# Attention output of a diffusion backbone: the two halves of a unit both copied by ScalarE and added on GpSimd

## Chip, core and metric

One core of one Trainium2 chip runs the whole program: TensorE (PE), VectorE (DVE), ScalarE (ACT), GpSimd (POOL), and SyncE (SP), which issues the DMAs. The metric is the device time of one execution in microseconds; three runs of the kernel before gave 2811.28 us as median (2810.51 to 2816.06).

## What is computed

Two layers over 512 latent tokens and 256 context tokens, 1024 wide. Each layer is a half-step SwiGLU, then three groups of heads side by side (GQA, a short gated convolution, MLA) between one input and one output projection, then another half-step SwiGLU; every sub-layer is modulated by a conditioning vector. The part that matters here is the attention, cut to its core:

```python
def one_block(qi):
    s = jnp.einsum('bhgqd,bhkd->bhgqk', qi, k).astype(jnp.float32) * scale
    p = jax.nn.softmax(s, axis=-1).astype(v.dtype)
    return jnp.einsum('bhgqk,bhkd->bhgqd', p, v)
```

There are 6 GQA heads and 6 MLA heads, each with values 64 wide. In layer 0 latent and context tokens are both queried, in layer 1 only the latent ones (`need_ctx`). All matrix products run in a split form: a float32 operand is held as a rounded high part and the remainder, and the products of the parts are summed.

## The kernel before

**Units.** The attention of a layer (`attend`, L1026) is a list of units: one head and two blocks of 128 queries. Layer 0 has three units a head (two of the latent tokens against all 768 keys, one of the context tokens against 256), so 36; layer 1 has two a head, so 24. A unit goes through these steps:

- `scores` (L945): queries times keys into a PSUM tile `ps`; `maxima` (L955): the row maximum, DVE, into a small tile `m`; `exps` (L960): ACT writes `t`, with the row sum.
- `transposes` (L967): PE turns the weights into PSUM tiles `po`; `high` (L985): ACT rounds them into `ph` or `s`; `low` (L998): DVE subtracts to get the remainder.
- `values` (L1007): PE multiplies by the values. The value operand holds a high and a low half side by side, so that the result `O`, a `po` tile of 128 partitions by 256, has the product with the high half in partitions 0 to 63 and that with the low half in 64 to 127.
- `out_copy` (L1014) and `out_add` (L1018) bring the two halves together: ACT copies partitions 64 to 127 of `O` into the tile `ot` of 64 by 256, and DVE adds it to partitions 0 to 63, read from PSUM, into the head's row `dest` of the mixed output (`mix`, an `s` tile).

Units overlap by three: in one turn of the loop the new unit's scores, the last one's transposes, the one before's `values` and the output of the one before that are issued. `jobs` hangs further work on given turns: `uq` and `ukv` (MLA's up projections, L1334 and L1362), `q_norm` and `k_norm` (L1408, L1427), `mla_part` (L1479), `mixnorm_a` and `mixnorm_b` (division by the row sums, L1457 and L1462) and `mix_split` (L1561).

**GpSimd's work in attention.** `q_norm` scales and rotates the MLA queries of all token tiles with seven GpSimd instructions for a latent tile and three for a context tile (L1417 to L1420, L1194, L1199, L1200), as soon as a chain of small DVE operations (`factors`, L1391) has made the scale `m`; `k_norm` does four more (L1432); `ukv` has short copies of the rotated key part `kr` (L1381); `mla_part` has the remainders `ql` and `s` (L1498), and `mix_split` those of the mixed rows (L1564).

**What sets the order.** In `attend` only TensorE is chained to program order (`chain("te")`, L1028). A scheduler places the instructions of ACT, DVE and POOL when the program is built, by its own estimate of when each may start; from then on every engine works through a fixed list in order. A tile with `bufs` buffers is written again when its last reader is done, and the writer waits for that by a semaphore. `ot` has two buffers (the tag is also used at the start by `wm0_copy`, L1639, for eight small copies), `po` has four, `ps` two.

**After the attention** come the output projection (`residual`, L373) and, beside it, the products for the modulation (`mod_steps`, L139; tiles `mr`, `mscr`) on DVE. Since helpers record most operations, their line is L65 in the profile.

Of the kernel before, what the change touches and what calls it, by code (L numbers as in the profile page):

```python
# [8 lines left out]
F32 = mybir.dt.float32  # L9
# [37 lines left out]
def tile_net(ctx: ExitStack, tc: tile.TileContext, a, out):  # L47
# [34 lines left out]
    te, ve, se, pe = Engine(nc.tensor, "te"), Engine(nc.vector, "ve"), Engine(nc.scalar, "se"), nc.gpsimd  # L82

    const = ctx.enter_context(tc.tile_pool(name="const", bufs=1))
    pool = ctx.enter_context(tc.tile_pool(name="pool", bufs=1))
# [4 lines left out]
    def nm(s):  # L90
        uid[0] += 1
        return f"{s}{uid[0]}"
# [4 lines left out]
    def temp(dt=F32, w=T):  # L97
        return pool.tile([P, w], dt, name=nm("t"), tag="t", bufs=NTMP)
# [838 lines left out]
    class Unit:  # L937
# [74 lines left out]
                te.matmul(out=self.O[:, :256], lhsT=self.V(kt), rhs=pl, start=False, stop=i == n - 1)  # L1012

        def out_copy(self):  # L1014
            self.tmp = pool.tile([64, 256], F32, name=nm("ot"), tag="ot", bufs=2)
            se.copy(self.tmp, self.O[64:128, :256])

        def out_add(self):  # L1018
            c = self.qbs[0] * P
            ve.tensor_add(self.dest[:, c:c + 256], self.O[0:64, :256], self.tmp)  # L1020

    class Nothing:
        def __getattr__(self, name):
# [576 lines left out]
    raws, parts, pms, sms = {}, {}, {}, {}  # L1600
# [36 lines left out]
                          start=kk == 0 and i == 0, stop=kk == KD - 1 and i == 1)  # L1637

    def wm0_copy(g):  # L1639
        sms[g] = pool.tile([64, 256], F32, name=nm("sm0"), tag="ot", bufs=2)  # L1640
        n = 2 if g in NATIVE else 4
        se.copy(sms[g][0:n, 0:256], pms[g][0:n, 0:256])

# [45 lines left out]
    Rs = pool.tile([P, D], F32, name="Rs", tag="mscr", bufs=1)  # L1689
    se.copy(Rs[:, LAT], Rl)  # L1690
    wm0_copy(0)
    wm0_high(1)
    for i in range(3):
        wm0_low(1, i)
    accs = []
    for g in range(KD):
        if g + 3 < KD:
            wm0_load(g + 3)
        if g:
            wm0_copy(g)  # L1700
        wm0_out(g)
        h.append((slot(F32R), slot(F32R)))
        cur = HMod(h[g], g, LAT, Rs, m01[1][:, g, 0:1], m01[0][:, g, 0:1], tv)
        cur.scaled()
        if g + 2 < KD:
            wm0_high(g + 2)
            cur.high()
            wm0_low(g + 2, 0)
            wm0_low(g + 2, 1)
            cur.low()  # L1710
            wm0_low(g + 2, 2)
        else:
            cur.high()
            cur.low()
        if g + 1 < KD:
            wm0_mm(g + 1)
        for j in PRE.get(g, ()):
            preload(j)
            accs.append(po())
        if g - 1 >= LAG:  # L1720
            for k in (range(g) if g - 1 == LAG else [g - 1]):
                for j in range(2):
                    lat_mm(accs[j], early[j], h, k, LAT, tv)
# [137 lines left out]
```

## Time and profile before

| | us |
|---|---|
| median of three runs | 2811.28 |
| the profiled execution | 2809.72 |
| its span | 2807.2 |
| first and last `ot` copy of layer 0 begin | 772.8, 953.3 |
| first and last `ot` copy of layer 1 begin | 2237.6, 2375.6 |
| POOL busy over the whole span | 189.6 |

The span is what the trace holds; 2.5 us lie around it. In a profile row stand the start and the length in us, the engine, the line, the operation, the tile written and the tiles read, and in square brackets how long the engine stood idle before it and who ended that. "Busy" counts the time in which an engine executes instructions. The chain of waits is followed back from the last instruction, at each step to what released it; its row by line gives the share of each kind of work on it.

### The profile page before, as it was taken

The page shows a single profiled execution, that of the slowest core. Times are in us where ns is not written, and L with a number is a line of the kernel's source. Part 1 is how long each engine was busy: PE and PEld are TensorE (multiplying, and loading weights), DVE is VectorE, ACT ScalarE, POOL GpSimd, SP SyncE. Part 2 cuts the span into 40 slices and gives each one's busy share as a digit, 9 for nine tenths or more (in the row PEclk, how much of TensorE's full clock was granted, in tenths as well). Part 3 has the DMA queues.
Part 4 walks back from the last instruction along what each step waited for, and adds up shares of the span by engine and source line. Part 5 has one row for each costly group of instructions (what it writes and reads, how often), then busy time and mean ns, then how long its engine had stood idle before and what let it go on. Part 6 is the DMA issues. An engine that isn't in the chain of part 4 may idle for free.

```text
span 2807.2 us, 38612 instructions
## 1 busy us (share of the span) xinstructions
PE 2691.4 (96%) x15188; PEld 2506.3 (89%) x15188; DVE 1983.7 (71%) x3391; ACT 1091.7 (39%) x1868; POOL 189.6 (7%) x225
## 2 busy tenths in 40 slices
PE   7999999989988999999999999999999899999999
PEld 4999999978878879999999899999988788888887
DVE  7657777787787887777777777776766888733333
ACT  5223333332477633333334333333333577422221
POOL 0000000011232210000000100000011233000000
PEclk9999999999999999999999999999999999999999
DMA  6423333224100331333333133333225101433232
GB/s 221 123 66 99 98 98 98 77 73 159 40 1 9 105 106 53 97 99 98 98 98 108 46 94 99 98 106 98 77 70 169 32 9 56 133 99 97 90 98 90
DMA packets 95461, 251.78 MB, mean 90 GB/s; under 512 B 11568, under 2 KB 41008, under 8 KB 95280
## 3 DMA queue, kind: packets, MB, share of 16 engines
q1 hardware_dynamic: 95280, 249.33, 28.6%
q8 instruction: 119, 1.95, 0.3%
q14 instruction: 62, 0.51, 0.1%
HBM read 247.19 MB, written 2.10 MB: 89 GB/s over the span
## 4 chain that ended last, share of the span: by engine, by line
PE 77%; DVE 12%; ACT 5%; DMA 3%; issue 2%; SPq 0%; POOL 0%; DVEq 0%; ACTq 0%
PE ps L65 45%; PE po L65 33%; DVE s L65 4%; DVE m L65 3%; ACT t L65 2%; ACT s L65 2%; DMA mr<-in_wm_dram 1%; DVE t L65 1%; DMA wr<-in_wiN_dram 1%; DVE wl L65 1%; DVE mr L65 1%; DVE mscr L65 1%; ACT ph L65 1%; DVE xT L65 0%; DMA s<-in_wm_dram 0%
## 5 line engine op out<-in xcount | busy, mean ns | idle before, releaser
L65 PE MATMUL ps<-s,wh 128*128 128x384 f32 (+2 forms) x4886 | 1185.5, 349 | 10.3 <-DVE xT L65 5.3
L65 PEld LDWEIGHTS ps<-s,wh 128*128 128x128 f32 x4886 | 868.8, 189 | 81.3 <-issue 5.7
L65 PE MATMUL ps<-s,wl 128*128 128x384 f32 (+2 forms) x2443 | 736.3, 350 | 0.9 <-DVE wl L65 0.8
L65 PE MATMUL po<-s,wh 128*128 128x384 f32 (+2 forms) x2538 | 668.5, 345 | 2.4 <-ACT t L65 1.7
L65 PEld LDWEIGHTS po<-s,wh 128*128 128x128 f32 x2538 | 462.4, 188 | 18.1 <-ACT t L65 2.7
L65 PEld LDWEIGHTS ps<-s,wl 128*128 128x128 f32 x2443 | 446.2, 189 | 33.3 <-DVE wl L65 2.6
L65 PE MATMUL po<-s,wl 128*128 128x384 f32 (+2 forms) x1269 | 437.5, 345 | 3.3 <-DVE wl L65 1.8
L65 ACT CAST wh<-wr 128x1024 fp32r<-128x1024 f32 (+4 forms) x239 | 219.9, 921 | 438.5 <-PE ps L65 299.2
L65 DVE TENSOR_TENSOR wl<-wr,wh 128x1024 fp32r<-128x1024 f32 (+5 forms) x229 | 243.1, 1064 | 174.5 <-ACT wh L65 172.3
L65 DVE SCALAR_TENSOR_TENSOR xT<-ps,mod,xT 128x256 f32<-128x256 f32 (+1 forms) x401 | 219.1, 588 | 195.0 <-PE ps L65 194.4
L65 PEld LDWEIGHTS po<-s,wl 128*128 128x128 f32 x1269 | 239.2, 188 | 11.7 <-DVE wl L65 2.4
L65 DVE SCALAR_TENSOR_TENSOR mr<-mr,sb 128x1024 f32<-128x1024 f32 x128 | 156.2, 1221 | 9.9 <-DMA mr<-in_wm_dram 9.1
L65 ACT COPY t<-po 128x384 f32<-128x384 f32 (+1 forms) x161 | 76.9, 478 | 199.5 <-PE po L65 196.7
L65 ACT ACTIVATE t<-t 128x384 f32<-128x384 f32 x106 | 55.7, 526 | 239.8 <-DVE t L65 239.8
L65 DVE TENSOR_TENSOR t<-ps,t 128x384 f32<-128x384 f32 (+3 forms) x91 | 55.2, 607 | 124.9 <-PE ps L65 124.6
L65 PE MATMUL po<-s,s 128*128 128x256 f32 (+2 forms) x856 | 132.1, 307 | 10.8 <-ACT s L65 3.9
L65 PEld LDWEIGHTS po<-s,s 128*128 128x128 f32 x856 | 121.3, 189 | 17.2 <-ACT s L65 5.8
L302 POOL TENSOR_TENSOR s<-s,t 128x256 f32<-128x256 f32 x15 | 12.6, 841 | 1746.1 <-ACT t L65 1676.3
L65 DVE TENSOR_TENSOR s<-t,s 128x768 fp32r<-128x768 f32 (+2 forms) x129 | 98.8, 767 | 38.7 <-ACT s L65 38.3
L65 DVE TENSOR_REDUCE m<-ps 128x1 f32<-128x768 f32 (+2 forms) x126 | 103.5, 821 | 31.0 <-PE ps L65 30.4
L65 DVE SCALAR_TENSOR_TENSOR mscr<-mr,sb 128x1024 f32<-128x1024 f32 x96 | 117.3, 1222 | 9.7 <-DMA mr<-in_wm_dram 8.0
L65 ACT CAST s<-t 128x768 fp32r<-128x768 f32 (+2 forms) x129 | 88.2, 684 | 89.1 <-DVE t L65 88.8
(168 smaller groups left out, 3208.3 us busy)
## 6 DMA issues: line engine op xcount, KB each, us to landing
mr<-in_wm_dram SPq DMA_DIRECT2D x128, 512.0 KB, 3.7
wr<-in_wg_dram SPq DMA_DIRECT2D x88, 512.0 KB, 3.5
wu<-in_wu_dram SPq DMA_DIRECT2D x53, 512.0 KB, 3.5
t<-in_wd_dram SPq DMA_DIRECT2D x56, 384.0 KB, 3.5
wr<-in_wu_dram SPq DMA_DIRECT2D x35, 512.0 KB, 3.5
wr<-in_wiT_dram SPq DMA_DIRECT2D x22, 512.0 KB, 3.7
wr<-in_wo_dram SPq DMA_DIRECT2D x14, 512.0 KB, 4.4
wr<-in_wd_dram SPq DMA_DIRECT2D x16, 448.0 KB, 3.2
```

The lines of the kernel that those rows point to most:

```text
L65: f(*args, **kw)
L302: (eng or ve).tensor_add(self.acc[:, :self.w], self.acc[:, :self.w], sq[:, :self.w])
```

## The change

`out_copy` copies both halves of `O` to SBUF with ACT, side by side into one `ot` tile of 64 by 512, and `out_add` adds the two halves of that tile on GpSimd (`pe`) in place of DVE. `ot` has one buffer in place of two, which takes the same room. `wm0_copy` at the start takes a `t` tile (five buffers) in place of an `ot` tile.

```diff
         def out_copy(self):
-            self.tmp = pool.tile([64, 256], F32, name=nm("ot"), tag="ot", bufs=2)
-            se.copy(self.tmp, self.O[64:128, :256])
+            self.tmp = pool.tile([64, 512], F32, name=nm("ot"), tag="ot", bufs=1)
+            for j in range(2):
+                se.copy(self.tmp[:, 256 * j:256 * j + 256], self.O[64 * j:64 * j + 64, :256])

         def out_add(self):
             c = self.qbs[0] * P
-            ve.tensor_add(self.dest[:, c:c + 256], self.O[0:64, :256], self.tmp)
+            pe.tensor_add(self.dest[:, c:c + 256], self.tmp[:, 0:256], self.tmp[:, 256:512])

     def wm0_copy(g):
-        sms[g] = pool.tile([64, 256], F32, name=nm("sm0"), tag="ot", bufs=2)
+        sms[g] = temp()
```

One line is added, so lines behind `out_copy` have a number higher by one in the changed kernel.

The scheduler's lists change with it. On GpSimd, in layer 0, the end of `q_norm`'s work read as follows before (s_6716, s_6759 and s_6784 are query tiles, g the gain, cosm a table, kr the key part):

```order
70 L1417 TENSOR_TENSOR s_6759<-s_6759,m_6910 128x6x64
71 L1200 TENSOR_TENSOR s_6716<-s_6716 128x6x32
72 L1419 TENSOR_TENSOR s_6759<-s_6759,m_6910 128x6x32
73 L1417 TENSOR_TENSOR s_6784<-s_6784,m_6910 128x6x64
74 L1420 TENSOR_TENSOR s_6759<-s_6759,g_5356 128x6x32
75 L1419 TENSOR_TENSOR s_6784<-s_6784,m_6910 128x6x32
```

The same place in the changed kernel; L1021 is the new addition, and ot_7201 is the output of layer 0's fourth unit:

```order
72 L1201 TENSOR_TENSOR s_6716<-s_6716 128x6x32
73 L1420 TENSOR_TENSOR s_6759<-s_6759,m_6910 128x6x32
74 L1382 COPY s_7148<-kr_6136 128x6x32
75 L1421 TENSOR_TENSOR s_6759<-s_6759,g_5356 128x6x32
76 L1418 TENSOR_TENSOR s_6784<-s_6784,m_6910 128x6x64
77 L1420 TENSOR_TENSOR s_6784<-s_6784,m_6910 128x6x32
78 L1021 TENSOR_TENSOR s_6619<-ot_7201 64x256
79 L1421 TENSOR_TENSOR s_6784<-s_6784,g_5356 128x6x32
```

The additions of units one to three stand ahead of `q_norm`'s first instruction (row 48, L1418), the fourth stands at row 78, behind 33 of `q_norm`'s 34 instructions (four rows count twice) and one copy. Layer 1 has the same picture: its fourth addition stands behind all of `q_norm`.

On ScalarE, in layer 0, the outputs of the fourth and the fifth unit were copied like this before:

```order
461 L65 COPY ot_7198<-po_7172 64x256
462 L65 CAST ph_7203<-po_7193 128x512
463 L65 ACTIVATE t_7206,rt_7187<-ps_7188,m_7200 128x768
464 L65 COPY s_7222<-ps_7209 128x6x64
465 L65 ACTIVATE t_7226<-ps_7209 128x384
466 L65 ACTIVATE s_7223<-ps_7209,m_6462 128x6x64
467 L65 ACTIVATE t_7237,rt_7187<-ps_7230,m_7235 128x768
468 L65 COPY ot_7263<-po_7239 64x256
469 L65 CAST s_7268<-po_7258 128x512
```

And in the changed kernel, with the engines whose semaphores an instruction waits for:

```order
464 L65 COPY ot_7201<-po_7175 64x256 [waits PE_49,Pool_49]
465 L65 COPY ot_7201<-po_7175 64x256
466 L65 CAST ph_7207<-po_7196 128x512 [waits PE_49]
467 L65 ACTIVATE t_7210,rt_7190<-ps_7191,m_7204 128x768 [waits DVE_49]
468 L65 COPY s_7226<-ps_7213 128x6x64 [waits PE_49]
469 L65 ACTIVATE t_7230<-ps_7213 128x384 [waits Activation_49]
470 L65 ACTIVATE s_7227<-ps_7213,m_6462 128x6x64
471 L65 ACTIVATE t_7241,rt_7190<-ps_7234,m_7239 128x768 [waits DVE_49,Activation_49]
472 L65 COPY ot_7267<-po_7243 64x256 [waits PE_49,Pool_49]
473 L65 COPY ot_7267<-po_7243 64x256
```

The sequence around them is the same; each copy has become two, and the first of a pair waits for GpSimd too.

On DVE, in layer 0, the last steps of the chain that makes `q_norm`'s scale m_6910 stood among other work before:

```order
917 L65 SCALAR_TENSOR_TENSOR m_6910<-m_6911,m_6910 128x72
918 L65 TENSOR_TENSOR s_6619<-po_7064,ot_7078 64x256
919 L65 TENSOR_TENSOR m_6911<-m_6910 128x72
920 L65 TENSOR_TENSOR s_7094<-po_7073,s_7093 128x512
921 L65 TENSOR_TENSOR m_6911<-m_6911,m_6909 128x72
922 L65 TENSOR_TENSOR s_7096<-po_7098,s_7095 128x512
923 L65 SCALAR_TENSOR_TENSOR m_6910<-m_6911,m_6910 128x72
924 L65 TENSOR_TENSOR m_6910<-m_6910,m_6905 128x72
```

In the changed kernel they stand together:

```order
915 L65 SCALAR_TENSOR_TENSOR m_6910<-m_6911,m_6910 128x72
916 L65 TENSOR_TENSOR m_6911<-m_6910 128x72
917 L65 TENSOR_TENSOR m_6911<-m_6911,m_6909 128x72
918 L65 SCALAR_TENSOR_TENSOR m_6910<-m_6911,m_6910 128x72
919 L65 TENSOR_TENSOR m_6910<-m_6910,m_6905 128x72
920 L65 TENSOR_TENSOR s_7097<-po_7075,s_7096 128x512
921 L65 TENSOR_TENSOR s_7099<-po_7101,s_7098 128x512
```

The addition is gone from DVE's list, and the two subtractions (128x512) have moved behind the chain. In layer 1 one of two subtractions and one addition leave this place. Elsewhere DVE and ACT change places of neighbours only. Beside the output projection of layer 0, 24 matmuls stand some 45 rows later on TensorE, and SP issues two loads of `mr` behind a weight load; in layer 1 four transposes and two weight loads change places with neighbours.

## Prediction

> **What bounds the kernel now.** First the page, then the two attention stages apart, since the change acts only there (and in eight small copies at the start). The page, of the whole span:
>
> ```profile
> span 2807.2 us, 38612 instructions
> PE 2691.4 (96%) x15188; PEld 2506.3 (89%) x15188; DVE 1983.7 (71%) x3391; ACT 1091.7 (39%) x1868; POOL 189.6 (7%) x225
> PE 77%; DVE 12%; ACT 5%; DMA 3%; issue 2%; SPq 0%; POOL 0%; DVEq 0%; ACTq 0%
> ```
>
> Over the span TensorE is the bound, ScalarE has room and GpSimd is idle. These are averages over stages. The busy time of each engine in the attention of layer 0, of layer 1, and in the MLA half of layer 0 alone (columns: stretch, length, PE, PEld, DVE, ACT, POOL, granted clock, DMA):
>
> ```profile
> 766.00:955.00 189.00, 163.31 (x1170) 149.88 (x1169) 155.05 (x316) 147.54 (x336) 56.42 (x64) 0.98 0.04 15
> 2230.00:2378.00 148.00, 136.02 (x969) 125.58 (x968) 128.64 (x258) 118.40 (x255) 46.69 (x55) 0.99 0.06 19
> 880.00:940.00 60.00, 56.20 (x426) 52.08 (x426) 50.57 (x87) 51.16 (x116) 16.26 (x9) 1.00 0.01 1
> ```
>
> Here three engines are busy 78 to 92% of the time, and none has much room. The chain of waits in the same two stages, by line, shows that they take turns:
>
> ```profile
> by line: PE po L65 24.8%; PE ps L65 17.2%; ACT t L65 16.9%; DVE m L65 10.3%; DVE s L65 8.5%; ACT ph L65 5.2%; ACT s L65 5.1%; issue 5.1%; ACT ot L65 2.2%; DVE pl L65 1.6%; ACT wh L65 0.9%; DVE wl L65 0.9%; DVE qh L65 0.6%; DVE mscr L65 0.6%
> by line: PE po L65 20.0%; DVE m L65 17.0%; ACT t L65 16.0%; PE ps L65 14.2%; DVE s L65 11.9%; ACT s L65 6.0%; issue 4.4%; ACT ph L65 3.1%; DVE pl L65 3.0%; ACT ot L65 1.8%; ACT wh L65 1.1%; DVE wl L65 0.8%; DVE mr L65 0.5%; DVE st L65 0.3%;
> ```
>
> So neither a microsecond taken from DVE nor one put on ACT counts in full, and neither is free. The two operations that the change touches, all 60 of each (nanoseconds shortest, median, longest):
>
> ```profile
> L65 ACT COPY ot<-po x60: 368/369/373, 772.8 to 2375.6; 64x256 f32<-64x256 f32 x60
> L65 DVE TENSOR_TENSOR s<-po,ot x60: 404/417/419, 777.0 to 2378.2; 64x256 f32<-64x256 f32 x60
> ```
>
> **The price of the new addition.** No GpSimd instruction of 64x256 is in the trace. The nearest are one of 128x256 (shortest, median, longest) and two that differ in partitions (us in total, ns of one):
>
> ```profile
> L302 POOL TENSOR_TENSOR s<-s,t x15: 722/738/1262, 588.3 to 2425.2; 128x256 f32<-128x256 f32 x15
> L1498 POOL TENSOR_TENSOR s<-t,s 96x768 fp32r<-96x768 f32 x6 | 11.0, 1838 | 30.1 <-DVE s L65 25.2 <-PE ps L65 5.0
> L1564 POOL TENSOR_TENSOR s<-s,s 128x768 fp32r<-128x768 f32 x6 | 10.9, 1835 | 6.7 <-ACT s L65 6.7
> ```
>
> 96 and 128 partitions take the same, so the width along a partition sets the time: 0.74 us, with 0.72 and 1.26 as ends.
>
> **Term 1, the wait in layer 0.** In GpSimd's new list the fourth unit's addition stands behind 33 of `q_norm`'s 34 instructions and a copy. With one `ot` buffer the fifth unit's copy must wait for that addition, and behind this copy ACT's list holds exponentials and rounded weights that PE waits for. The first of those GpSimd instructions, the last one ahead of the addition's place, and the copy now moved ahead of it; then ACT's fifth copy and the first exponential that waits behind it:
>
> ```profile
> 794.99 0.83 POOL L1417 TENSOR_TENSOR s<-s,m 128x384 f32<-128x384 f32 x1 [14.85 <-DVE m L65]
> ...
> 812.07 0.50 POOL L1419 TENSOR_TENSOR s<-s,m 128x192 f32<-128x192 f32 x1
> 812.52 0.33 POOL L1381 COPY s<-kr 128x192 f32<-128x192 f32 x1
> ```
>
> ```profile
> 803.18 0.37 ACT L65 COPY ot<-po 64x256 f32<-64x256 f32 x1
> ...
> 814.55 0.48 ACT L65 ACTIVATE t<-ps,m 128x256 f32<-128x256 f32 x1 [2.21 <-DVE m L65]
> ```
>
> GpSimd gets there at 812.57 + 0.33 = 812.9 if it starts at 794.99. It may start sooner, since two subtractions and an addition have left the chain on DVE that it waits for; one of the subtractions, the chain's end, and a product of a small tile with itself that comes later in this stage; below it one of its like:
>
> ```profile
> 792.87 0.69 DVE L65 TENSOR_TENSOR s<-po,s 128x512 fp32r<-128x512 f32 x1 [0.94 <-ACT s L65]
> ...
> 794.67 0.23 DVE L65 TENSOR_TENSOR m<-m,m 128x72 f32<-128x72 f32 x1
> ...
> 810.23 2.40 DVE L65 TENSOR_TENSOR m<-m 128x4 f32<-128x4 f32 x1
> ```
>
> ```profile
> L65 DVE TENSOR_TENSOR m<-m 128x2 f32<-128x2 f32 x1 | 0.2, 151 | 0.0
> ```
>
> I take 2 x 0.69 + 0.42 = 1.8 us sooner (ends: 0, and 2.7 with the wait of 0.94). The addition then ends at 812.9 - 1.8 + 0.74 = 811.8, 8.7 us behind 803.18. Of this something comes back: the product of 128x4 took 2.40 us where its like took 0.151, and ended at 812.63, when GpSimd's back-to-back work paused (812.57); ACT idled 2.21 us for it. ACT now stands during that time anyway, so 2.2 come back: 6.5.
>
> [...]
>
> While ACT stands, PE will stand too, some 7 us. What that does to the granted clock (eighth column), after stretches with PE busy 4.89 of 10 and 2.03 of 5 us:
>
> ```profile
> 850.00:860.00 10.00, 4.89 (x39) 4.38 (x38) 9.04 (x29) 6.12 (x13) 0.00 (x0) 0.98 0.01 2
> 860.00:864.00 4.00, 4.00 (x22) 3.94 (x21) 2.59 (x7) 2.51 (x9) 1.81 (x1) 0.62 0.37 131
> 2270.00:2275.00 5.00, 2.03 (x16) 1.59 (x14) 4.86 (x13) 1.28 (x5) 2.06 (x5) 1.00 0.00 0
> 2275.00:2278.00 3.00, 2.57 (x13) 2.51 (x14) 3.00 (x12) 1.80 (x4) 0.00 (x0) 0.70 0.00 0
> 2278.00:2281.00 3.00, 3.00 (x14) 2.96 (x14) 1.57 (x6) 1.51 (x4) 2.07 (x3) 0.73 0.00 0
> ```
>
> 4 us at 0.62 lose 1.5, 6 us at some 0.72 lose 1.7: I add 1.5. **Term 1 is +8.0.** Low end: 7.7 us of wait, ACT catching up 22% of the next 12.7 us (its idle share above), no clock loss: 4.9. High end: 812.9 + 1.26 - 803.18 + 1.7 = 12.7.
>
> **Term 2, the wait in layer 1.** The same picture, on GpSimd, ACT and DVE:
>
> ```profile
> 2256.91 0.83 POOL L1417 TENSOR_TENSOR s<-s,m 128x384 f32<-128x384 f32 x1 [12.73 <-DVE m L65]
> ...
> 2270.95 0.61 POOL L1200 TENSOR_TENSOR s<-s 128x192 f32<-128x192 f32 x1
> 2271.51 0.62 POOL L1381 COPY s<-kr 128x192 f32<-128x192 f32 x2
> ```
>
> ```profile
> 2265.60 0.37 ACT L65 COPY ot<-po 64x256 f32<-64x256 f32 x1 [0.30 <-PE po L65]
> ...
> 2274.86 0.90 ACT L65 ACTIVATE t<-ps,m 128x768 f32<-128x768 f32 x1 [3.72 <-DVE m L65]
> ```
>
> ```profile
> 2256.03 0.68 DVE L65 TENSOR_TENSOR s<-po,s 128x512 fp32r<-128x512 f32 x1
> ...
> 2267.21 3.68 DVE L65 TENSOR_TENSOR m<-m 128x4 f32<-128x4 f32 x1
> ```
>
> Behind all of `q_norm` (2271.56) and one copy (0.31), 1.1 sooner by a subtraction and an addition, plus 0.74: 2271.5, or 5.9 behind 2265.60. DVE's blocked product stands at the same time and cost ACT 3.72 before, of which 3.5 come back. The clock loss is there already. **Term 2 is +2.4** (ends 0 and 2271.87 + 1.26 - 2265.60 = 7.5).
>
> **Term 3, 60 more copies on ACT:** 60 x 0.369 = 22.1 us. Of the old copies 2.2% of 189 and 1.8% of 148 us are on the chain, 4.2 + 2.7 = 6.9 of 22.1, 18 or 19 of 60. For the new ones I take the same share: **+6.8** (ends 0 and 22.1).
>
> **Term 4, 60 additions gone from DVE:** 60 x 0.417 = 25.0 us. On the chain stand 9 of layer 0's and 11 of layer 1's, here the first and the last of each:
>
> ```profile
> 777.10 0.32 DVE s L65
> ...
> 953.99 0.76 DVE s L65 x2
> ...
> 2240.51 0.42 DVE s L65
> ...
> 2378.21 0.43 DVE s L65
> ```
>
> 20 x 0.417 = 8.3: **-8.3** (ends 0 and -25.0). `O` is freed by ACT's second copy now, which the same rows price: where DVE was late it is sooner, where it was prompt 0.37 later.
>
> **Term 5, the rest: +1.0.** Outside the two waits one buffer suffices: pair of copies, addition, next copy take 0.37 + 0.37 + 0.74 = 1.5 us, 3.3 if one GpSimd instruction of 1.84 is in between, and the closest copies ahead of the last units are 2.95 apart:
>
> ```profile
> 889.05 0.37 ACT L65 COPY ot<-po 64x256 f32<-64x256 f32 x1
> 892.00 0.37 ACT L65 COPY ot<-po 64x256 f32<-64x256 f32 x1
> ```
>
> At each layer's end the last output comes 0.37 + 0.74 - 0.42 = 0.7 later; the output projection takes that row last, which hides most: 0.5 for both. 0.5 more is for short DVE products that meet one of the additions (up to 4). The eight copies at the start take one of five `t` buffers, whose last readers are done, and a few matmuls and loads that change places bring no work: 0. The cover there is that the work is the same in another order; without it, a load that comes late is allowed for by the far end of 4.
>
> **Sum:** 8.0 + 2.4 + 6.8 - 8.3 + 1.0 = 9.9 us on the profiled execution's 2809.72, so 2819.6. The median of the runs is 1.56 above that execution: **2821.2 us**. The measurement can tell about 0.2% (5.6 us) from no change; the three runs spread over as much.
>
> **Rivals.** *DVE was the bound (faster).* If DVE's relief counts nearly everywhere, 41 of 60 additions (-17.1), with half of term 3 (+3.4), term 1 at its low end (+4.9) and the rest 0, it is -8.8: 2802.5. For it: DVE ends 22% and 33% of the two chains, and `O` waits for it. Against: in the MLA half PE is busy 56.20 of 60. It decides from some 30 additions on the chain, where I count 20. *The waits dissolve (same).* Term 1 at 4.9, term 2 at 0, term 3 at 3.4, term 4 at -8.3: 0.0, 2811.3. For it: ACT has 22% of idle time to catch up in. It is also what comes out if the additions find GpSimd free sooner than the rows say. *ACT becomes the bound (slower still).* In the MLA half some 12 copies of 0.37 (36 units in 180 us) bring ACT from 51.16 to 55.6 of 60, beside PE's 56.20; if 44 of 60 new copies count (+16.2), the sum is 19.3: 2830.6. *The additions hold DVE up (slower still).* If each of the 60 holds a DVE product for half its 0.74 us, that is 22.2 us, of which 28%, DVE's mean share of the two chains, are 6.2 on the sum: 2827.4. For it: the two long products. Against: most of DVE's work here reads PSUM (`po`, `ps`), and the subtractions beside GpSimd's busy stretch took 0.68 and 0.69.
>
> **Chances.** My forecast 0.42; ACT the bound 0.20; DVE held up 0.05; the waits dissolve 0.19; DVE was the bound 0.14. Slower by over 0.2%: 0.42 + 0.20 + 0.05 = 0.67; within 0.2%: 0.19; faster: 0.14. The range reaches from just under the second rival to just above the third, 2808 to 2833; the faster one and the far ends of terms 1 and 3 together are left out.
>
> **What would show it.** Right: in layer 0 ACT idle for some 8 us ahead of the fifth pair of copies, released by POOL, PE idle beside it and a granted clock near 0.6 behind it; in layer 1 about 6 us, with the 128x4 product no longer followed by a wait of ACT; GpSimd additions of some 0.74 us; elsewhere pairs of copies without a wait for POOL. Wrong: pairs of copies that never wait for POOL (terms 1 and 2), MLA units longer by 0.3 us or more each (term 3 too small), or units of the first half shorter by more than 0.4 us (term 4 too small).

## The result and the profile after

The changed kernel takes **2821.68 us** (median of 6 runs, 2819.77 to 2823.87); the kernel before, beside it on the same chip, 2811.28 (6 runs, 2809.52 to 2816.06). The ratio is 1.0036, with a 95% interval of 1.0026 to 1.0046: slower by 10.4 us, where 9.9 were predicted. The page of the changed kernel, and the two stretches that answer to the attention of layer 0 and of layer 1 before (same columns):

```profile
span 2822.1 us, 38725 instructions
...
PE 2690.1 (95%) x15188; PEld 2504.8 (89%) x15188; DVE 1965.5 (70%) x3331; ACT 1108.7 (39%) x1928; POOL 233.9 (8%) x285
```

```profile
770.00:972.00 202.00, 169.56 (x1190) 154.54 (x1189) 148.39 (x286) 158.65 (x374) 82.86 (x100) 0.97 0.04 14
2242.00:2396.00 154.00, 138.33 (x979) 128.11 (x977) 123.00 (x239) 124.99 (x279) 64.55 (x80) 0.98 0.07 22
```

DVE lost 18 us of work, ACT gained 17, POOL 44, and PE has as much as before. What is new over the span is time in which PE stands: 2822.1 - 2690.1 = 132.0 us (115.8 before). In the two stretches it is 202.00 - 169.56 = 32.4 us in layer 0 (25.7 before) and 15.7 in layer 1 (12.0 before). The stretches themselves grew by 13 and 6 us; the rest of that is PE being busy longer in them, with 20 and 10 more matmuls and a granted clock lower by 0.01. The chain of waits breaks off early in this trace, so its shares can't be set beside those of before. The tile view of `ot` names one cause. Its rows are the copies, the additions (shortest, median, longest; first and last start), and those who waited (us in all, times):

```profile
L65 ACT COPY ot<-po x120: 351/369/386, 776.4 to 2393.9; 64x256 f32<-64x256 f32 x120
L1021 POOL TENSOR_TENSOR s<-ot x60: 716/729/1342, 777.2 to 2394.3; 64x256 f32<-64x256 f32 x60
...
  ACT ot L65: 18.1, 5
```

An addition takes 0.73 us on GpSimd (VectorE took 0.417 in the trace of before). ScalarE waited for one five times, 18.1 us together. The two long waits are where the prediction put them. Layer 0, on ACT, POOL, PE and DVE:

```profile
806.06 0.19 ACT L65 ACTIVATION_READ_ACCUMULATOR t<-ps,m 128x1 f32 x1
814.78 0.75 ACT L65 COPY ot<-po 64x256 f32<-64x256 f32 x2 [8.53 <-POOL s L1021]
```

```profile
796.10 0.83 POOL L1418 TENSOR_TENSOR s<-s,m 128x384 f32<-128x384 f32 x1 [1.72 <-DVE m L65]
...
814.03 0.72 POOL L1021 TENSOR_TENSOR s<-ot 64x256 f32<-64x256 f32 x1
```

```profile
817.08 1.65 PE L65 MATMUL ps<-k,s 128*128 128x512 f32 x4 [7.35 <-ACT t L65]
```

```profile
821.76 0.15 DVE L65 TENSOR_TENSOR m<-m 128x4 f32<-128x4 f32 x1
```

The fifth pair of copies waits 8.53 us for the fourth addition, PE 7.35 us for the exponential behind that pair, and the product of 128x4 that took 2.40 us before takes 0.15. The clock behind the wait (eighth column, as before):

```profile
810.00:813.00 3.00, 0.00 (x0) 0.00 (x0) 0.00 (x0) 0.00 (x0) 3.00 (x7) 1.00 0.00 0
813.00:816.00 3.00, 0.00 (x0) 0.00 (x0) 0.00 (x0) 1.19 (x3) 2.84 (x7) 0.51 0.00 0
816.00:819.00 3.00, 1.92 (x7) 1.73 (x8) 1.61 (x3) 2.75 (x7) 1.13 (x3) 0.50 0.05 11
819.00:822.00 3.00, 2.62 (x17) 2.22 (x16) 2.87 (x7) 2.34 (x7) 0.07 (x1) 0.85 0.01 3
```

Half clock for some 7 us, of which PE stood in the first four. Layer 1, on ACT, POOL and DVE:

```profile
2284.44 0.75 ACT L65 COPY ot<-po 64x256 f32<-64x256 f32 x2 [6.13 <-POOL s L1021]
```

```profile
2283.70 0.72 POOL L1021 TENSOR_TENSOR s<-ot 64x256 f32<-64x256 f32 x1
```

```profile
2284.45 0.69 DVE L65 TENSOR_TENSOR s<-s,po 128x512 f32<-128x512 f32 x1 [6.66 <-POOL s L1021]
```

Here two engines wait for the same addition: ACT for the buffer, and DVE for the sum itself. DVE's product is `mixnorm_b`'s, which scales the finished rows; the prediction had not seen this second waiter.

To place the rest I take the start of the first copy of each of the 60 units in each trace and subtract its start in before (us; a stretch's entry is the growth of that difference from its first to its last unit; units 1 to 36 are layer 0, 37 to 60 layer 1). The last four columns are kernels of the next section:

| units | changed | VectorE relieved alone | copies added alone | two units as before | middle units only |
|---|---|---|---|---|---|
| 4 to 8 (first wait) | +6.3 | -2.7 | +1.6 | -1.8 | +0.7 |
| 8 to 18 | -1.0 | -1.1 | -0.7 | -2.6 | -1.0 |
| 18 to 30 (MLA) | +2.9 | +0.1 | +0.6 | +2.9 | +0.5 |
| 30 to 36 | +4.3 | +0.1 | +3.3 | +5.1 | +1.2 |
| 40 to 45 (second wait) | +2.1 | +2.8 | 0.0 | -2.3 | -4.2 |
| 45 to 55 | -1.1 | -3.6 | -1.5 | -1.2 | -1.1 |
| 55 to 60 | +4.1 | -0.2 | +2.5 | +4.1 | +2.3 |

Single entries carry chance of up to 2 us (last section), and what a layer's last units lose is partly won back behind them (the changed kernel's first copy is 15.35 us late in unit 36 and 11.80 in unit 37). The profiled executions differ by 14.15 us, more than the medians, because the first copy already starts 3.5 us later (776.4 against 772.8). Over the fourteen profiles of this study the first copy starts between 770.87 and 777.52, and the two earliest belong to kernels that have the two copies in the first units as well (runs 4 and 7), so these 3.5 us are not put down to the change.

The MLA stretch (18 to 30) holds a third wait, shorter and in four places, which the prediction does not have. `mla_part` has GpSimd form the remainder of a head's keys, and PE's weight loads need it. In the changed kernel an addition stands ahead of it in GpSimd's list; on POOL and PE, and below them the same remainder before:

```profile
883.95 0.73 POOL L1021 TENSOR_TENSOR s<-ot 64x256 f32<-64x256 f32 x1 [2.98 <-ACT ot L65]
884.76 1.85 POOL L1499 TENSOR_TENSOR s<-t,s 96x768 fp32r<-96x768 f32 x1
```

```profile
886.66 0.19 PEld L65 LDWEIGHTS ps<-s,qh 96*128 96x128 f32 x1 [0.66 <-POOL s L1499]
```

```profile
875.55 1.85 POOL L1498 TENSOR_TENSOR s<-t,s 96x768 fp32r<-96x768 f32 x1 [4.11 <-DVE s L65]
```

Before, GpSimd was idle when DVE had the rounded part ready (for 3.5 to 4.1 us ahead of these four remainders), and no weight load waited for a remainder. Set side by side, the starts of the same weight loads in the two traces fall apart by 0.4 to 0.6 us more at each of the four waits, 2.0 of the 2.9 us of the stretch.

### The profile page after: what moved, and what is told of

Read it like the earlier page. It is cut to its first block, busy times and chain, and to the rows that moved or that the text cites. A ratio compares the mean times of both kernels' runs of the same rounds, so it can differ in the third digit from the quotient of the medians.

```text
span 2822.1 us, 38725 instructions
## 1 busy us (share of the span) xinstructions
PE 2690.1 (95%) x15188; PEld 2504.8 (89%) x15188; DVE 1965.5 (70%) x3331; ACT 1108.7 (39%) x1928; POOL 233.9 (8%) x285
## 5 line engine op out<-in xcount | busy, mean ns | idle before, releaser
L65 PEld LDWEIGHTS po<-s,wh 128*128 128x128 f32 x2538 | 461.6, 188 | 18.1 <-ACT t L65 2.7
```

Of the source, the lines that this page charges most:

```text
L65: f(*args, **kw)
```

## The experiments

Each ran 5 to 11 times beside the kernel before, whose medians there were 2812.16, 2812.09 and 2811.97 us (for the first, second and third four kernels, each four on a chip of their own); ratios are to these. "The lower half" is `O[0:64]`. All but the two that say so are edits of the changed kernel, so units "as before" in them still have its one buffer.

**1. Two buffers again, addition in place**

```diff
-self.tmp = pool.tile([64, 512], ..., tag="ot", bufs=1)
-for j in range(2):
-    se.copy(self.tmp[:, 256 * j:256 * j + 256], self.O[64 * j:64 * j + 64, :256])
+self.tmp = pool.tile([P, 256], ..., tag="ot", bufs=2)[o:o + 64, :]   # o = 64 * (head % 2)
+se.copy(self.dest[:, c:c + 256], self.O[0:64, :256])
+se.copy(self.tmp, self.O[64:128, :256])
...
-pe.tensor_add(self.dest[:, c:c + 256], self.tmp[:, 0:256], self.tmp[:, 256:512])
+pe.tensor_add(self.dest[:, c:c + 256], self.dest[:, c:c + 256], self.tmp)
```

> The changed kernel, but ScalarE copies the lower half straight into the destination and only the upper half into a 64x256 buffer, of which there are two again; GpSimd adds in place, at the same places of its list. Theory A (the two waits for the one buffer carry the loss, terms 1 and 2): the fifth pair of copies no longer waits in either layer; in layer 0 the sixth pair waits some 2 us for the fourth addition, in layer 1 none. About 8 us come back: 2813.5 us (2811 to 2816). Theory B (ScalarE's 60 more copies carry it): nothing comes back, 2819 to 2823.

Measured: 2824.35 us, ratio 1.0045 (1.0032 to 1.0057). Nothing came back, against theory A, and the number by itself is nearer to theory B; but the rows show waits. The wait had moved and not gone, in layer 0 (ACT) and in layer 1 (DVE):

```profile
813.98 0.37 ACT L65 COPY ot<-po 64x256 f32<-64x256 f32 x1 [4.77 <-POOL s L1022]
```

```profile
2283.57 0.69 DVE L65 TENSOR_TENSOR s<-s,po 128x512 f32<-128x512 f32 x1 [6.56 <-POOL s L1022]
```

The sixth pair waits 4.77 us instead of the fifth 8.53, and in layer 1 DVE's product still needs the late sum. So the single buffer is not the cause by itself: with two, the addition's place behind `q_norm` still makes others wait. The MLA units were also longer here, 3.8 us from unit 18 to 30 instead of 2.9, with the copies of each unit in another order; of this PE falls back 2.3 us instead of 2.0 at the weight loads that wait for `mla_part`'s remainder, and the rest was not tried.

**2. Only the start** (the kernel before with one line of the change)

```diff
-sms[g] = pool.tile([64, 256], F32, name=nm("sm0"), tag="ot", bufs=2)
+sms[g] = temp()
```

> The kernel before, with the eight small copies of the start put into the work buffers, nothing else. Theory A (the start costs nothing, the 2 us by which the changed kernel's profile is late at 588 us are this one execution's): 2811.3 us within 1. Theory C (these copies hold up a buffer or a load at the start): 2813 to 2814.

Measured: 2812.45 us, ratio 0.9998 (0.9989 to 1.0007). The start costs nothing; theory C falls.

**3. The additions back on VectorE, from SBUF**

```diff
-pe.tensor_add(self.dest[:, c:c + 256], self.tmp[:, 0:256], self.tmp[:, 256:512])
+ve.tensor_add(self.dest[:, c:c + 256], self.tmp[:, 0:256], self.tmp[:, 256:512])
```

> The changed kernel with the additions back on VectorE, which now reads both halves from SBUF: so the kernel before plus 60 copies on ScalarE, and one buffer. No pair waits long for the one buffer. Theory A (18 or 19 of the 60 copies count): 2818 us (2815 to 2821). Theory B (ScalarE is the bound of the stage, 44 or more count): 2827 or more. If ScalarE's spare time takes them all: 2811.3.

Measured: 2822.54 us, ratio 1.0036 (1.0021 to 1.0051), above theory A's range and below B's; but the kernel held something neither had counted. An addition of two SBUF halves met GpSimd's work, on DVE, then POOL and DVE in the MLA half:

```profile
808.07 7.53 DVE L65 TENSOR_TENSOR s<-ot 64x256 f32<-64x256 f32 x1
```

```profile
899.78 1.84 POOL L1499 TENSOR_TENSOR s<-t,s 96x768 fp32r<-96x768 f32 x1 [3.51 <-DVE s L65]
```

```profile
900.02 1.87 DVE L65 TENSOR_TENSOR s<-ot 64x256 f32<-64x256 f32 x1
```

An addition that takes 0.42 us took 7.53 beside `q_norm`, and 1.2 to 1.9 in ten other places of layer 0. So this run does not price the copies; run 9 does.

**4. The first six additions of each layer on VectorE**

```diff
-pe.tensor_add(...)
+(ve if self.n < 6 else pe).tensor_add(...)        # self.n: the unit's number in its layer
```

> The changed kernel with the additions of the first six units of each layer on VectorE, the other 48 on GpSimd; one buffer. Theory A (terms 1 and 2, together 10.4 us, go, and 12 additions come back to VectorE, a third of them on the chain, 1.7 us): 2813 us (2810 to 2816), the product of 128x4 again followed by a wait of ScalarE of some 2 and 3.7 us. Theory B (ScalarE's copies carry the loss): 2820 or more.

Measured: 2808.88 us, ratio 0.9987 (0.9978 to 0.9996): 12.8 us less than the changed kernel, 1 us below theory A's range, and faster than before although an addition of 7.55 us is in layer 0 of this kernel too (its rows are in the last section). Theory A's sign did not come in layer 1: the product of 128x4 is short there, on DVE

```profile
2271.77 0.18 DVE L65 TENSOR_TENSOR m<-m 128x4 f32<-128x4 f32 x1
```

instead of 3.68 us. In the table's terms this trace loses 5.1 us from unit 4 to 8 and gains 4.2 from 40 to 45, so the short product may be what makes it faster than before; that was not tried apart.

**5. VectorE relieved and nothing else** (the kernel before)

```diff
-se.copy(self.tmp, self.O[64:128, :256])
+se.copy(self.dest[:, c:c + 256], self.O[64:128, :256])
...
-ve.tensor_add(self.dest[:, c:c + 256], self.O[0:64, :256], self.tmp)
```

> The kernel before without its 60 additions: ScalarE copies the upper half straight into the destination, the lower half is left out of the output. Still one copy for each unit and nothing on GpSimd, so this is term 4 alone. As predicted (20 of 60 additions on the chain): 2812.2 - 8.3 = 2804 us (2801 to 2807). If VectorE was the bound (41 or more of 60): 2795 or less. If its relief is worth nothing: 2811 to 2813.

Measured: 2804.02 us, ratio 0.9969 (0.9957 to 0.9981): 8.1 us faster, where term 4 was -8.3. VectorE was not the bound.

**6, 7, 8. The change for some units alone**

```diff
-for j in range(2):
+for j in range(2) if self.new else (1,):
...
+if self.new:
     pe.tensor_add(self.dest[:, c:c + 256], self.tmp[:, 0:256], self.tmp[:, 256:512])
+else:
+    ve.tensor_add(self.dest[:, c:c + 256], self.O[0:64, :256], self.tmp[:, 256:512])
...
+u.new = n >= 6                      # 6; 7: n < 6; 8: n >= len(units) // 2
```

> The change for all units but the first six of each layer, which stay as before (one copy, VectorE adds from PSUM). No addition stands behind the scaling of the queries, no pair of copies waits for GpSimd there, and no VectorE addition of SBUF halves can be locked out by it. If the first six units carry the whole loss: faster than the run with the first six additions on VectorE from SBUF by what the 7 us lock cost there, 2803 us (2800 to 2807). If the loss is spread over the units: 2815 or more.

> The opposite part: only the first six units of each layer are changed, the other 48 stay as before; one buffer. If the two waits carry the loss: 2812.2 + 10 to 16, 2822 to 2828 us, with waits of some 8 and 6 us for the fourth addition as in the changed kernel. If the loss is spread: 2812 to 2816.

> The change in the second half of each layer's units alone (18 and 12 of them, the MLA heads). In the changed kernel's trace these units are 0.17 to 0.25 us longer each in layer 0 than before and 0.1 us shorter each in layer 1. If that is the copies on the chain: 2814 to 2816 us. If it is hidden in what follows the attention: 2811 to 2813. If VectorE's relief counts more: below 2810.

Measured: the late 48 units alone 2813.78 us, ratio 1.0004 (0.9996 to 1.0013); the first six of each layer alone 2818.31, ratio 1.0020 (1.0011 to 1.0030); the MLA units alone 2815.52, ratio 1.0009 (1.0000 to 1.0018). The first six units of each layer carry most of the loss, 6 of 10 us, though less than I expected of them; the other 48 units together gain nothing, where I expected 9: the MLA units alone lose 3.4 (0 to 5). The late units alone are 5 us slower than run 4, which differs only in how the first six are added; why is open. The traces do not place it in the first six units: from unit 1 to 8 run 4 loses 4.4 us and the late units' kernel gains 0.2.

**9. The copies alone**

```diff
-pe.tensor_add(self.dest[:, c:c + 256], self.tmp[:, 0:256], self.tmp[:, 256:512])
+ve.tensor_add(self.dest[:, c:c + 256], self.O[0:64, :256], self.tmp[:, 256:512])
```

> The kernel before plus a copy of each unit's lower half by ScalarE that nobody reads; VectorE still adds from PSUM. So this is term 3 alone, without any GpSimd addition and without an addition of two SBUF halves. As predicted (18 or 19 of 60 copies on the chain): 2812.1 + 6.8 = 2819 us (2816 to 2821). If ScalarE is the bound (44 or more): 2828. If the idle time of ScalarE takes them: 2811 to 2813.

Measured: 2813.86 us, ratio 1.0008 (0.9999 to 1.0017): some 1.9 us, at most 4.8, where term 3 was 6.8. (For the one buffer ScalarE waited once, 1.4 us.)

**10. Run 4, with the last five units of each layer as before**

```diff
+u.how = "sbuf" if n < 6 else "before" if n >= len(units) - 5 else "changed"
```

(`before`: one copy, VectorE adds from PSUM; `sbuf`: two copies, VectorE adds from SBUF; `changed`: two copies, GpSimd adds.)

> The run with the first six additions on VectorE from SBUF (2808.9 us), with the last five units of each layer as before too. If the late last outputs of the layers cost what the shifts of the last five pairs show (some 2 us in layer 0, 4 in layer 1): 2803 to 2805 us. If the output projection hides them, as predicted (0.5): 2808 to 2809.

Measured: 2812.78 us, ratio 0.9997 (0.9988 to 1.0006). The last pairs came earlier (units 55 to 60: +2.3 instead of +4.1) and the time did not fall, so nothing shows that the late last pairs cost time. It rose by 3.9 us against run 4, outside both expectations; why is open.

**11. The change where the table shows a gain**

```diff
+u.how = (("before", "sbuf")[len(units) == 24] if n < 6 else
+         "changed" if n < 18 or n == 18 and len(units) == 24 else "before")
```

> The change only where the traces show it to gain: in layer 0 units 7 to 18, in layer 1 units 7 to 19; the first six of layer 1 copy both halves and add on VectorE, all others stay as before. By the sums of the steps of the pairs of copies (layer 0 -1, layer 1 -3 and -1): 2807 us (2804 to 2809). If steps read off single traces don't add up: 2810 to 2814.

Measured: 2804.30 us, ratio 0.9967 (0.9955 to 0.9980), 7.7 us faster than before and better than both kernels, at the lower end of the expected range. The largest gain in the table is again units 40 to 45 (-4.2), where the product of 128x4 took 0.20 us as in run 4; one remainder of `mla_part` still waits behind an addition. By the tile view 25 additions are left on GpSimd; six of VectorE's read two SBUF halves, the longest 0.885 us:

```profile
L1022 POOL TENSOR_TENSOR s<-ot x25: 717/728/741, 816.4 to 2352.0; 64x256 f32<-64x256 f32 x25
L65 DVE TENSOR_TENSOR s<-ot x6: 409/415/885, 2242.9 to 2278.4; 64x256 f32<-64x256 f32 x6
```

**12. The fourth and the fifth unit as before, 56 changed** (the edit of run 6 with `n not in (3, 4)`)

> The changed kernel with the fourth and the fifth unit of each layer as before, the other 56 changed: nothing waits behind the scaling of the queries, so what is gone against the changed kernel (2821.7 us) is the two waits. As predicted (8.0 and 2.4): 2811.3 us (2809 to 2813). By the runs with the six first units one way and the other (6 to 8): 2814 to 2816. If the waits cost little because ScalarE catches up: 2819 or more.

Measured: 2813.37 us, ratio 1.0002 (0.9993 to 1.0011). This lies between the two expectations. Without the two waits the change costs at most 3 us. How long ACT still waits for an addition (us, times; from the tile view), and DVE's products of 128x4:

```profile
  ACT ot L65: 3.0, 2
```

```profile
812.81 1.53 DVE L65 TENSOR_TENSOR m<-m 128x4 f32<-128x4 f32 x1
...
2273.25 4.32 DVE L65 TENSOR_TENSOR m<-m 128x4 f32<-128x4 f32 x1
```

18.1 us of ScalarE's waiting have become 3.0, and the long products are back, as the sums of terms 1 and 2 had it.

## Why the prediction was right, step by step

**Term 1 (predicted +8.0).** The wait was 8.53 us (8.7). `q_norm` started 1.1 us later than before while the third pair was 2.6 us late, so 1.5 sooner (1.8). The 2.2 us came back: the seventh pair has regained 2.3. Against before, units 4 to 8 lose 6.3 us; half clock lay over the end of the stall, and the 1.5 us that I added for it are already in these 6.3. But the relief of VectorE and the copies are in them too. Against run 12, which has those and not the wait, the same step is 6.3 + 1.8 = 8.1 us, as predicted; single traces do not tell the two readings apart.

**Term 2 (+2.4).** The wait was 6.13 us (5.9), 3.0 came back over the next two units (3.5), 2.95 stayed (against run 12 the step is 2.1 + 2.3 = 4.4). The size is about right; the mechanism was half of it, since DVE waits for the sum as well. Run 1 shows the difference: a second buffer does not help.

**Both waits together (10.4)** are what run 12 takes away: with each kernel set against the kernel before that ran beside it, 10.40 - 1.40 = 9.0 us, or 0.34 points of the two ratios, 9.6 us. So the two waits are most of the 10.4 us that the change costs, as predicted.

**Term 4 (-8.3)** was measured by itself: -8.1. That fits twenty additions of 60 on the chain; the interval allows 13 to 29. (Run 5 also frees `O` with the copy, sooner than DVE did; that was not tried apart.) The first rival (41 of 60, -17.1) is excluded by the interval of run 5 (-12.1 to -5.3 us).

**Term 3 (+6.8)** is the step that failed, as a term by itself: run 9 gives +1.9 (-0.3 to +4.8). I had taken the share of the old copies on the chain, 18 or 19 of 60, for the new ones; by run 9 it is 5, by the far end of its interval 13. Yet with the relief, the copies and the additions on GpSimd all in (run 12: +1.4) the time is near the predicted -0.5 of terms 3 to 5, and far from 1.9 - 8.1 = -6.2: from run 5 to run 12 it rises by 9.35 us for 56 more copies and the additions on GpSimd. So what the sum lacked is in the additions, or in copies that cost more once VectorE is relieved. Part of it can be placed. In the MLA stretch from unit 18 to 30 the table has relief alone +0.1, copies alone +0.6, all together +2.9, and of these 2.9 us PE falls back 2.0 at the four weight loads that wait for `mla_part`'s remainder. The waits go with the additions: runs 4, 6, 10 and 12 have the same four and grow by 2.9 there, run 8 has three and grows by 2.2, run 11 one and 0.5, and runs 2, 5, 7 and 9 have none and change by -0.3 to +0.6. Before and changed from unit 17 to 30:

```profile
868.96:930.87 61.91, 57.74 (x437) 53.46 (x436) 51.91 (x89) 52.22 (x120) 16.56 (x9) 1.00 0.00 1
```

```profile
877.13:941.92 64.79, 59.33 (x439) 53.87 (x438) 48.77 (x76) 55.81 (x135) 25.91 (x22) 1.00 0.01 1
```

DVE gives up 3.1 us, ACT takes 3.6 more, POOL 9.4, and the stretch is 2.9 longer. That ScalarE's copies cost more beside a relieved VectorE, because they no longer fall into time in which others wait for VectorE, is a reading that would account for the rest; it is not shown, since relieved VectorE with two copies and no addition was not run. So the last step of the prediction, 0.5 us from the forecast, owes something to luck: term 3 was some 5 us too large for the copies alone, and what the additions do to GpSimd's own work, which the sum put at nothing, filled part of the gap.

**Term 5 (+1.0).** The start is worth nothing (run 2), and no cost of the layers' ends shows (run 10), though one buffer did not quite suffice there: ScalarE's other three waits for an addition (0.39, 0.50 and 2.58 us) stand at the last pairs of the layers. That the rest of GpSimd's list bears the additions at no cost was assumed and is wrong for `mla_part`, as above. The third part, DVE's products beside the additions, is in the rows of DVE in the MLA half (units 17 to 33), before and changed (us in all, ns of one):

```profile
L65 DVE TENSOR_TENSOR pl<-po,ph 128x512 fp32r<-128x512 f32 x20 | 13.2, 685 | 0.8 <-ACT ph L65 0.3
...
L65 DVE CAST qh<-t 96x768 fp32r<-96x768 f32 x5 | 2.8, 556 | 1.9 <-ACT t L65 1.5
...
L65 DVE TENSOR_TENSOR wl<-wo,wh 128x1024 fp32r<-128x1024 f32 x1 | 2.2, 2212 | 0.0
```

```profile
L65 DVE TENSOR_TENSOR pl<-po,ph 128x512 fp32r<-128x512 f32 x20 | 13.3, 685 | 2.6 <-ACT ph L65 2.1
...
L65 DVE CAST qh<-t 96x768 fp32r<-96x768 f32 x5 | 3.1, 612 | 6.6 <-ACT t L65 6.6
L65 DVE TENSOR_TENSOR wl<-wo,wh 128x1024 fp32r<-128x1024 f32 x1 | 2.8, 2818 | 0.0
```

Instructions that read PSUM hardly changed (`pl` took 685 ns in both); the one product of two SBUF operands in this stretch and some casts did, by 0.9 us in 80. The 0.5 us that the sum has for products meeting an addition are shown by no run; in their place the rows show these 0.9 us of longer instructions. Over the attention of both layers, an estimate: what DVE's longer instructions (by over 0.1 us) take beyond the median of their form in all runs is 8.7 us in all before and 8.4 in the changed kernel. So the additions do not hold VectorE up as the last rival needs (6.2 us).

**The other rivals.** That the waits dissolve is excluded by runs 7 and 12. That ScalarE becomes the bound is excluded as a whole (44 copies would have cost 16.2 us), though part of the 9.35 us between runs 5 and 12 may be copies on the chain.

## What to carry to other kernels

Before work moves to an idle engine, read what stands in that engine's list at the place: 0.73 us of addition kept ScalarE waiting 8.5 us because it stood behind 18 us of other work, and everyone who needs the result waits, whether for the buffer or for the sum. Read as well what will stand behind the new work: the engine was idle on average, and yet its own remainders came late for PE. When one edit relieves an engine and loads another, price both together or each in turn; shares of the chain belong to the kernel and the operations that they were read from. And test the edit by places: the change that loses 10 us on all 60 units wins 8 on 25 of them, with six more that only copy both halves.

## What the runs showed of the hardware

**A VectorE addition of two SBUF halves took 7.55 us beside a run of GpSimd instructions.** In run 4, on DVE, and on POOL the first and the last ones that began meanwhile:

```profile
802.76 7.55 DVE L65 TENSOR_TENSOR s<-ot 64x256 f32<-64x256 f32 x1
```

```profile
803.19 0.60 POOL L1201 TENSOR_TENSOR s<-s,cosm 128x192 f32<-128x192 f32 x1
...
809.14 0.34 POOL L1383 COPY s<-kr 128x192 f32<-128x192 f32 x1
809.44 0.58 POOL L1422 TENSOR_TENSOR s<-s,g 128x192 f32<-128x192 f32 x1
809.97 0.89 POOL L1383 COPY s<-kr 128x64 f32<-128x64 f32 x3
```

Twelve GpSimd instructions of two operands began while the addition ran; it ended at 810.31, when GpSimd had come to its row of copies; it had not ended with the single copy at 809.14. In run 3 the same addition took 1.87 us beside one instruction of 1.84 us; in run 4, with GpSimd working back to back, the one instruction became a dozen. It need not take so long: in layer 1 of the same run, on DVE and POOL,

```profile
2265.18 0.86 DVE L65 TENSOR_TENSOR s<-ot 64x256 f32<-64x256 f32 x1
```

```profile
2265.16 0.60 POOL L1422 TENSOR_TENSOR s<-s,g 128x192 f32<-128x192 f32 x1
2265.72 0.78 POOL L1201 TENSOR_TENSOR s<-s,cosm 128x192 f32<-128x192 f32 x1
```

the addition was through after 0.86 us, and the GpSimd instruction that began meanwhile took 0.78 instead of 0.60. What decides between the two is not shown here. With one operand in PSUM none of the 60 additions of before took more than 0.419 us.

**The same gaps, two clocks.** A stretch of PE work ahead of the first copies, before and changed, with the same instructions and the same gaps of PE within 0.02 us:

```profile
754.41 0.96 PE L65 MATMUL ps<-k,s 128*128 128x512 f32 x4 [1.61 <-ACT t L65]
```

```profile
756.62 0.97 PE L65 MATMUL ps<-k,s 128*128 128x512 f32 x4 [1.63 <-ACT t L65]
```

```profile
754.00:757.00 3.00, 2.47 (x15) 2.18 (x16) 1.58 (x3) 1.97 (x5) 0.00 (x0) 1.00 0.00 0
757.00:760.00 3.00, 3.00 (x25) 2.91 (x24) 1.20 (x3) 2.25 (x6) 0.00 (x0) 1.00 0.01 3
```

```profile
756.20:759.20 3.00, 2.46 (x13) 2.17 (x14) 1.57 (x3) 1.69 (x5) 0.00 (x0) 0.88 0.00 0
759.20:762.20 3.00, 3.00 (x14) 2.92 (x14) 0.10 (x1) 1.13 (x3) 0.00 (x0) 0.55 0.01 3
```

One execution kept its full clock and the other lost (0.12 + 0.45) x 3 = 1.7 us of it, an estimate from these rows; why the two differ is not shown here. A single trace therefore can't price an edit to better than such a loss, and the entries of the table above are read with that in mind; the verdicts rest on the medians.
